# Differential attention: the low queries' score product as two row tiles, and a reordered finish of the attention outputs

## The chip, the cores and the metric

The kernel runs on one core of one Trainium2 chip. Its time is the device time in microseconds (us) of that core for one execution. A core has five engines with queues of their own that run at the same time and wait for each other through semaphores: TensorE (PE in the profile; its weight loads are listed apart as PEld), VectorE (DVE), ScalarE (ACT), GpSimd (POOL) and SyncE (SP), which here issues all DMAs.

## The reference

One layer of a hybrid block over 1024 latent tokens and 256 context tokens of width 1024: a modulated RMS norm, one wide input projection, a gated linear attention (GLA), a differential attention, and a merge with an output projection. The change lies in the differential attention, 8 heads of 2 x 64 query and key channels and 128 value channels:

```python
s1 = einsum('bhqd,bhkd->bhqk', qb1, k1) * scale      # d = 64, 1280 keys
s2 = einsum('bhqd,bhkd->bhqk', qb2, k2) * scale
a = softmax(s1) - lam * softmax(s2)
o = einsum('bhqk,bhkv->bhqv', a, v)                  # 128 value channels
...
b = rms_norm(o_diff) * diff_gain * (1 - lam_init) * silu(diff_gate)
```

Each of the two score maps of a head is called a component below (comp 0 and 1).

## The kernel before

**Split numbers.** A float32 operand is split into a high part of type fp32r and a low part, the rest. A product of two split operands is three matmuls: high x high, high x low and low x high (`mm3`). For the scores the contraction is only 64 deep, so the 128 rows of the array hold both parts of the keys: rows 0 to 63 the high part, rows 64 to 127 the low part, and the same query part stands in both halves. Two matmuls then give (Kh + Kl)Qh and (Kh + Kl)Ql. `score` in `att_scores` issues them for j = 0 (high queries) and j = 1 (low queries).

**A unit.** The attention runs over 64 units: 8 heads (hd) by 8 blocks of 128 queries (qt). For each unit `att_scores` issues, for each component, two blocks of 512 keys (`MAIN`) with two matmuls each, and for both components together one block of 256 keys each (`TAIL`), again two matmuls each: 8 matmuls of 128x512 and 4 of 128x256. They write the PSUM tile `s5`. Then `att_max` takes the row maximum on DVE, `att_exp` the exponential on ACT with the sum in `z`, and `att_mix` joins the two maps on DVE. `att_tr` transposes the result on PE, ten 128x128 transposes; `split2` makes high and low parts on ACT, POOL and DVE; `att_av` multiplies by the values for two units at a time (a pair, pr), 30 matmuls of 128x256; `att_fin` finishes a pair.

**The finish.** `att_fin` copies a pair's 128x256 output from PSUM on ACT, transposes it on PE back to tokens, squares it on ACT with a sum, multiplies it by the gate (tile `g`, loaded from `d_dg`) on DVE, works out the norm's scale (two small DVE steps, a power on POOL), scales it on DVE, transposes it again on PE, copies it on ACT and stores it to `d_bT`. Its tiles in SBUF are named `b1k`, those in PSUM `b1` (shown as `b` in the profile).

**Fill work.** `fill` runs matmuls of other products (tiles `mb` and `h`, `wt`), which the attention does not need, between the attention's own.

**Order.** Nothing is ordered by hand except the turns of scores, transposes and value products (`att_order`). A planner written in the kernel (`Driver`) simulates the engines with a cost for each operation while the program is built; generators are resumed when their operands would be ready, and the order in which they emit instructions is the order in the engines' queues. The cost of a matmul in the planner is set in `mm`.

**Keys.** `att_keys` loads a head's keys, for each component high and low part, into a ring of three slots (`kk`) of the tile `hk` (from `d_kT`), by two DMAs of 64 rows by 1280 columns. Two slots come free when a head's last unit has issued its scores.

All matmuls of `mm` carry line 349 in the profile, all transposes line 375, all DMAs line 314, and all operations of ACT, DVE and POOL line 201; so groups are told apart by their tiles.

Of the kernel before, what the change touches and what calls it, by code (L numbers as in the profile page):

```python
# [13 lines left out]
AF = mybir.ActivationFunctionType  # L14
ALU = mybir.AluOpType
# [5 lines left out]
P = 128  # L21
# [3 lines left out]
T = S + CTX  # L25
NK = D // P
EPS = 1e-6
# [205 lines left out]
class Hybrid:  # L233
# [111 lines left out]
            yield  # L345
        self.d.spawn(later(), AtPE(at), prio=-9)

    def mm(self, out, lhsT, rhs, start, stop, more=False):
        self.ins = self.nc.tensor.matmul(out, lhsT, rhs, start=start, stop=stop, skip_group_check=more).ins  # L349
        n = rhs.free_size()  # L350
        c = 0.009 + max(n, 230) * 0.000428 if rhs.dtype == F32R else 0.006 + max(4 * n, 470) / 2400
        return self.d.op("PE", c, [out], [lhsT, rhs])

    def mm3(self, out, sh, sl, mh, ml, first, last, more=False):
        self.mm(out, sh, mh, first, False, more)
# [1492 lines left out]
    def att_keys(self):  # L1848

        for hd in range(8):  # L1850
            c, x = hd // 4, hd % 4
            for i in range(10):
                yield self.ev_st["dk", c, i]
            if hd:
                yield self.ev_q[0, 1]
            else:
                yield self.gla_free[3]
                yield from self.acq("hc", 16)
                Driver.places = (T, 2 * T, 3 * T)
                self.hk = self.t("hk", [P, HK], F32R)  # L1860
            K = []
            for comp in range(2):
                rows = slice(64 * comp, 64 * comp + 64)
                yield from self.acq("kk")
                m = (2 * hd + comp) % 3
                kt = self.hk[:, m * T:(m + 1) * T]
                self.dma(kt[0:64], self.d_kT[0][c][x, rows])
                self.dma(kt[64:128], self.d_kT[1][c][x, rows])
                K.append(kt)
            self.K[hd] = K  # L1870
            self.d.set(self.ev_k[hd], self.d.when(*K))
# [68 lines left out]
    def att_scores(self):  # L1940

        nc, d = self.nc, self.d
        yield self.ev_b
        s5 = self.t("s5", [P, 2 * T])
        for hd in range(8):
            for qt in range(8):
                pr, qs = qt // 2, slice((qt % 2) * P, (qt % 2) * P + P)
                yield self.ev_k[hd]
                yield self.ev_q[hd, pr]
                K, Q = self.K[hd], self.Q[hd, pr]  # L1950

                def score(po, comp, o, n):
                    bank = po.offset % (2 * T) // 512
                    for j in range(2):
                        e = self.mm(po, Q[comp][:, j, qs], K[comp][:, o:o + n], j == 0, j == 1)
                        self.banked(self.ins, "PE", bank)
                    return e

                u = dict(hd=hd, qt=qt, E=[None, None], mt=self.t("sm", [P, 2]), mx=[self.t("sm", [P, 1]) for _ in range(2)],
                         z=self.t("sm", [P, 2]), left=2, ev=[Event() for _ in range(3)])  # L1960

                for comp in range(2):
                    yield from self.acq(f"s{comp}")
                    pm = s5[:, 1536 * comp:1536 * comp + 1024]
                    if comp == 0:
                        yield from self.turn("S", 8 * hd + qt, 0)
                    if self.flush:
                        self.flush(1)
                    for x, (o, n) in enumerate(self.MAIN[comp]):
                        e = score(pm[:, x * 512:(x + 1) * 512], comp, o, n)  # L1970
                        if x == 0:
                            yield AtPE(0)
                    self.passed("S", 8 * hd + qt, comp)
                    d.spawn(self.att_max(u["ev"][comp], u["mx"][comp], pm, 3 * comp, 3 * comp + 1), On(e, "DVE"), prio=-3)
                    yield AtPE(0)
                    if comp == 0:
                        yield from self.acq("st")
                        yield from self.turn("S", 8 * hd + qt, 1)
                        pt = s5[:, 1024:1536].rearrange("p (c k) -> p c k", c=2)
                        for x in range(2):  # L1980
                            e = score(pt[:, x], x, *self.TAIL[x])
# [36 lines left out]
    def att_mix(self, u):  # L2018
        d = self.d
        x = u["qt"] % 2  # L2020
        cf = self.t("sm", [P, 1])
        E, z = u["E"], u["z"]
        self.dve.reciprocal(cf, z[:, 1:2])
        yield On(self.dve.tensor_scalar(cf, cf, z[:, 0:1], self.nlam, ALU.mult, ALU.mult), "DVE")
        if x in self.PC:
            self.pool.tensor_scalar(E[1], E[1], cf, 0.0, ALU.mult, ALU.add)
            e = self.pool.tensor_tensor(E[0], E[0], E[1], ALU.add)
        else:
            e = self.dve.scalar_tensor_tensor(E[0], E[1], cf, E[0], ALU.mult, ALU.add)
        self.att[u["hd"], u["qt"]] = (E[0], z)  # L2030
        self.rel("e5", e)
        d.set(self.ev_a[u["hd"], u["qt"]], e)


    TAIL = ((1024, 256), (0, 256))
    MAIN = (((0, 512), (512, 512)), ((256, 512), (768, 512)))
    GROUPS = ((0, 4), (4, 4), (8, 2))
# [30 lines left out]
    def att_av(self):  # L2068
        d = self.d
        for hd in range(8):  # L2070
            for pr in range(4):
# [29 lines left out]
                d.spawn(self.att_fin(hd, pr, po, [self.att[hd, 2 * pr + x][1] for x in range(2)]), On(e, "ACT"),  # L2101
                        prio=-5 if hd == 7 and pr > 1 else self.PF)
                yield AtPE(0)

# [35 lines left out]
        self.rel("ac", e)  # L2140
        return e

    def att_fin(self, hd, pr, po, zs):
# [6 lines left out]
        ot = self.t("b1k", [P, 256])  # L2150
        e = self.act.activation(ot, po, AF.Copy)
        self.rel(self.PO, e)
        z2 = self.t("sm", [P, 2])
        for x in range(2):
            self.dve.tensor_scalar(z2[:, x:x + 1], zs[x][:, 0:1], zs[x][:, 0:1], EPS, ALU.mult, ALU.mult)
        yield AtPE(e)
        yield from self.acq("b1k")
        yield from self.acq("b1")
        pt = self.t("b1", [P, 2, P])
        for x in range(2):  # L2160
            e = self.tr(pt[:, x], ot[:, x * P:(x + 1) * P])
        self.rel("b1k", e)
        yield On(e, "ACT")
        oo = self.t("b1k", [P, 2, P])
        ss = self.t("sm", [P, 2])
        for x in range(2):
            e = self.act.activation(oo[:, x], pt[:, x], AF.Square, accum_out=ss[:, x:x + 1])
        yield d.on("DVE", pt, g)
        e2 = self.dve.tensor_tensor(g, pt, g, ALU.mult)
        self.rel("b1", max(e, e2))  # L2170
        yield On(e, "DVE")
        for x in range(2):
            self.dve.tensor_scalar(ss[:, x:x + 1], ss[:, x:x + 1], 1.0 / P, z2[:, x:x + 1], ALU.mult, ALU.add)
        yield d.on("POOL", ss)
        yield On(self.pool.tensor_tensor(ss, ss, self.nhalf[:, 0:2], ALU.pow), "DVE")
        for x in range(2):
            e = self.dve.tensor_scalar(oo[:, x], g[:, x], ss[:, x:x + 1], None, ALU.mult)
        self.rel("b1k", e)
        yield AtPE(e)
        yield from self.acq("b1k")  # L2180
        yield from self.acq("b1")
        pb = self.t("b1", [P, 2, P])
        for x in range(2):
            e = self.tr(pb[:, x], oo[:, x])
# [626 lines left out]
```

## Time and profile before

| | us |
|---|---|
| median of 3 runs | 1616.22 |
| lowest, highest | 1616.01, 1618.52 |
| span of the profiled execution | 1614.1 |
| attention with its fill work, about 890 to 1450 us of the span | 560 |
| VectorE busy in the whole span | 1224.4 (76%) |
| ScalarE busy | 835.7 (52%) |
| GpSimd busy | 634.3 (39%) |

The span is that of one execution, from its first to its last instruction. Busy times are unions: while one matmul is still draining and the next has begun, the time counts once, so TensorE can show as busy through a short wait, and a matmul's own duration (about 400 ns for 512 columns) is longer than its distance to the next one. The distance from start to start is what a matmul costs in a dense stream; it is read from the timeline or from the chain. In a row, "128\*128 128x512 f32 x496 | 138.4, 399 | 1.8" means 128 rows by 128 columns of the array in use, an output of 128x512, 496 instructions, 138.4 us busy in all, 399 ns mean of one, and 1.8 us of idle engine before them.

### The profile page before, as it was taken

The numbers are of one execution on the slowest core, as the hardware profiler recorded it, in microseconds if no ns is written. First come the engines' busy times: TensorE is split into PE (matmuls) and PEld (weight loads), VectorE is DVE, ScalarE is ACT, GpSimd is POOL, SyncE is SP. The second block draws the span as 40 slices with busy tenths as digits, with TensorE's granted clock in tenths as the row PEclk, the third lists the DMA queues.
The fourth block names the chain that finished last, engine by engine and source line by source line (L and its number), as shares of the span: only waits on it lengthen the run. The fifth ranks groups of instructions, "written<-read, shape, count | busy, mean of one in ns | idle before, by whom it ended". The sixth has DMA issues, their size and how long they took to land.

```text
span 1614.1 us, 24349 instructions
## 1 busy us (share of the span) xinstructions
PE 1591.4 (99%) x8229; PEld 1328.1 (82%) x8229; DVE 1224.4 (76%) x2118; ACT 835.7 (52%) x1720; POOL 634.3 (39%) x663
## 2 busy tenths in 40 slices
PE   8999999999999999999999999999999999999999
PEld 3788888888888888888888788888888888888887
DVE  4787945676777779767677688878778888888994
ACT  4776523435343454555535566665665666656331
POOL 1500000001415667535564256656765666560000
PEclk9999999999999999999999999999999999999999
DMA  8576996998878367564645944545587545347662
GB/s 305 201 257 239 329 304 232 344 331 295 278 238 281 116 194 235 167 212 118 189 118 158 253 121 121 151 129 151 150 264 218 159 137 150 111 155 285 204 206 100
DMA packets 259565, 331.16 MB, mean 205 GB/s; under 512 B 22600, under 2 KB 160752, under 8 KB 259440
## 3 DMA queue, kind: packets, MB, share of 16 engines
q1 hardware_dynamic: 259440, 329.60, 63.8%
q8 instruction: 65, 1.06, 0.3%
q14 instruction: 60, 0.49, 0.1%
HBM read 225.20 MB, written 104.33 MB: 204 GB/s over the span
## 4 chain that ended last, share of the span: by engine, by line
PE 89%; DVE 4%; issue 2%; DMA 2%; ACT 1%; POOL 1%; SPq 0%; ACTq 0%; DVEq 0%; POOLq 0%
PE mm L349 30%; PE mb L349 11%; PE s L349 8%; PE mc L349 7%; PE b L349 6%; PE tp L349 5%; PE gt L349 5%; PE b L375 5%; PE go L349 4%; PE gs L349 4%; PE mz L349 2%; PE tp L375 2%; DVE sm L201 1%; POOL at L201 1%; DMA w<-in_w_ada 1%
## 5 line engine op out<-in xcount | busy, mean ns | idle before, releaser
L349 PE MATMUL mm<-w,h 128*128 128x512 f32 x912 | 231.0, 400 | 0.0
L349 PE MATMUL mb<-h,wt 128*128 128x512 f32 x840 | 223.0, 400 | 0.0
L201 DVE TENSOR_REDUCE sm<-s 128x1 f32<-128x1024 f32 (+1 forms) x192 | 193.3, 1037 | 10.7 <-PE s L349 6.6
L201 ACT ACTIVATE e<-s,sm 128x1280 f32<-128x1280 f32 x128 | 169.3, 1329 | 54.4 <-DVE sm L201 51.2
L349 PEld LDWEIGHTS mm<-w,h 128*128 128x128 f32 x912 | 167.4, 188 | 32.8
L201 POOL TENSOR_TENSOR at<-ac,at 128x512 fp32r<-128x512 f32 x128 | 188.2, 1471 | 10.7
L349 PEld LDWEIGHTS mb<-h,wt 128*128 128x128 f32 x840 | 151.4, 188 | 28.6 <-DVE ft L201 0.3
L201 POOL TENSOR_SCALAR at<-ac 128x512 fp32r<-128x512 f32 x128 | 96.9, 757 | 191.0 <-ACT ac L201 190.7
L349 PE MATMUL s<-hk,aq 128*128 128x512 f32 x744 | 169.0, 363 | 1.9 <-ACT e L201 1.8
L349 PE MATMUL mm<-h,w 128*128 128x512 f32 x672 | 168.2, 400 | 1.0 <-DVE h L201 1.0
L349 PEld LDWEIGHTS mm<-h,w 128*128 128x128 f32 x672 | 123.7, 188 | 26.4 <-DVE h L201 1.5
L201 DVE TENSOR_TENSOR w<-raw,w 128x512 fp32r<-128x512 f32 x128 | 96.0, 766 | 54.2 <-ACT w L201 52.0
L349 PEld LDWEIGHTS s<-hk,aq 128*128 128x128 f32 x744 | 117.7, 189 | 18.5 <-ACT e L201 3.6
L349 PE MATMUL b<-at,vv 128*128 128x256 f32 x960 | 130.1, 287 | 1.1 <-ACT ac L201 0.8
L349 PEld LDWEIGHTS b<-at,vv 128*128 128x128 f32 x960 | 119.5, 191 | 2.8 <-ACT ac L201 1.0
L201 ACT ACTIVATE w<-raw 128x512 fp32r<-128x512 f32 x128 | 78.1, 626 | 84.2 <-PE tp L349 23.8
L201 ACT ACTIVATE ac<-b 128x512 f32<-128x512 f32 x122 | 72.5, 598 | 91.8 <-PE b L375 91.7
L201 POOL TENSOR_TENSOR sm<-sm,nhalf 128x2 f32<-128x2 f32 (+2 forms) x94 | 107.7, 1146 | 27.9 <-DVE sm L201 22.7
L201 DVE SCALAR_TENSOR_TENSOR e<-e,sm,e 128x1280 f32<-128x1280 f32 x64 | 117.9, 1842 | 1.0
L349 PE MATMUL mm<-w,g 128*128 128x512 f32 x432 | 105.7, 389 | 0.0
L349 PEld LDWEIGHTS mm<-w,g 128*128 128x128 f32 x432 | 81.1, 188 | 16.9
L375 PE MATMUL b<-ident,e 128*128 128x128 f32 x610 | 92.6, 273 | 1.3 <-ACT ac L201 0.8
(357 smaller groups left out, 3054.2 us busy)
## 6 DMA issues: line engine op xcount, KB each, us to landing
raw<-in_w_in SPq DMA_DIRECT2D x62, 512.0 KB, 4.3
g<-d_s SPq DMA_DIRECT2D x32, 640.0 KB, 6.2
g<-d_s SPq DMA_DIRECT2D x32, 512.0 KB, 5.7
aq<-d_qT SPq DMA_DIRECT2D x124, 128.0 KB, 3.4
d_dv<-pl SPq DMA_DIRECT2D x40, 256.0 KB, 3.9
gv<-d_v SPq DMA_DIRECT2D x40, 256.0 KB, 3.3
d_kT<-pl SPq DMA_DIRECT2D x40, 256.0 KB, 2.8
hk<-d_kT SPq DMA_DIRECT2D x32, 320.0 KB, 5.9
```

The lines of the kernel that those rows point to most:

```text
L201: self.ins = f(out, *args, **kw).ins
L349: self.ins = self.nc.tensor.matmul(out, lhsT, rhs, start=start, stop=stop, skip_group_check=more).ins
L375: self.nc.tensor.transpose(out, src, self.ident[:n, :n])
```

## The change

Two edits, both in the attention.

1. For each unit and component the two matmuls with the high queries come first, for both blocks of 512 keys, over all 128 rows as before. The two with the low queries use 64 rows each: the first block rows 0 to 63, the second rows 64 to 127. So that both multiply the keys' high part, `att_keys` loads high and low parts the other way round in the columns from `SWAP[comp]` on (512 for comp 0, 768 for comp 1), which makes four DMAs for two per component. The product of the low queries with the keys' low part is left out for these blocks. The planner counts the first of the two 64-row matmuls as free. The `TAIL` blocks stay as they were, with 128 rows.
2. In `att_fin` ACT copies the transposed output from PSUM to SBUF once, both squares read that copy, and one DVE step per half multiplies by scale and gate, where there was one product with the gate and two scalings. The two sums of the exponentials of a pair lie in one tile (`zp`), so two pairs of small DVE steps become one each.

```diff
-    def mm(self, out, lhsT, rhs, start, stop, more=False):
+    def mm(self, out, lhsT, rhs, start, stop, more=False, cost=1.0):
...
-        return self.d.op("PE", c, [out], [lhsT, rhs])
+        return self.d.op("PE", c * cost, [out], [lhsT, rhs])
...
-                self.dma(kt[0:64], self.d_kT[0][c][x, rows])
-                self.dma(kt[64:128], self.d_kT[1][c][x, rows])
+                for j in range(2):
+                    for h, cs in ((j, slice(0, self.SWAP[comp])), (1 - j, slice(self.SWAP[comp], T))):
+                        self.dma(kt[64 * h:64 * h + 64, cs], self.d_kT[j][c][x, rows, cs])
...
-                def score(po, comp, o, n):
-                    bank = po.offset % (2 * T) // 512
-                    for j in range(2):
-                        e = self.mm(po, Q[comp][:, j, qs], K[comp][:, o:o + n], j == 0, j == 1)
-                        self.banked(self.ins, "PE", bank)
+                def score(po, comp, o, n, j, rows=slice(0, P), cost=1.0):
+                    e = self.mm(po, Q[comp][rows, j, qs], K[comp][rows, o:o + n], j == 0, j == 1, cost=cost)
+                    self.banked(self.ins, "PE", po.offset % (2 * T) // 512)
                     return e
...
                     for x, (o, n) in enumerate(self.MAIN[comp]):
-                        e = score(pm[:, x * 512:(x + 1) * 512], comp, o, n)
+                        score(pm[:, x * 512:(x + 1) * 512], comp, o, n, 0)
                         if x == 0:
                             yield AtPE(0)
+                    for x, (o, n) in enumerate(self.MAIN[comp]):
+                        e = score(pm[:, x * 512:(x + 1) * 512], comp, o, n, 1, slice(64 * x, 64 * x + 64), float(x))
...
+    SWAP = (512, 768)
...
-        for x in range(2):
-            self.dve.tensor_scalar(z2[:, x:x + 1], zs[x][:, 0:1], zs[x][:, 0:1], EPS, ALU.mult, ALU.mult)
+        self.dve.scalar_tensor_tensor(z2, zp[:, :, 0], EPS, zp[:, :, 0], ALU.mult, ALU.mult)
...
-        oo = self.t("b1k", [P, 2, P])
-        ss = self.t("sm", [P, 2])
+        oc = self.t("b1k", [P, 2, P])
+        ss = self.t("sm", [P, 2])
+        self.rel("b1", self.act.activation(oc, pt, AF.Copy))
         for x in range(2):
-            e = self.act.activation(oo[:, x], pt[:, x], AF.Square, accum_out=ss[:, x:x + 1])
-        yield d.on("DVE", pt, g)
-        e2 = self.dve.tensor_tensor(g, pt, g, ALU.mult)
-        self.rel("b1", max(e, e2))
+            e = self.act.activation(ot[:, x], oc[:, x], AF.Square, accum_out=ss[:, x:x + 1])
...
-        for x in range(2):
-            self.dve.tensor_scalar(ss[:, x:x + 1], ss[:, x:x + 1], 1.0 / P, z2[:, x:x + 1], ALU.mult, ALU.add)
+        self.dve.scalar_tensor_tensor(ss, ss, 1.0 / P, z2, ALU.mult, ALU.add)
...
         for x in range(2):
-            e = self.dve.tensor_scalar(oo[:, x], g[:, x], ss[:, x:x + 1], None, ALU.mult)
+            e = self.dve.scalar_tensor_tensor(oc[:, x], oc[:, x], ss[:, x:x + 1], g[:, x], ALU.mult, ALU.mult)
```

More of the change, by code (lines that the diff above doesn't have):

```diff
@@ L1950, in att_scores @@
                 K, Q = self.K[hd], self.Q[hd, pr]
-                def score(po, comp, o, n):
-                    bank = po.offset % (2 * T) // 512
-                    for j in range(2):
-                        e = self.mm(po, Q[comp][:, j, qs], K[comp][:, o:o + n], j == 0, j == 1)
-                        self.banked(self.ins, "PE", bank)
-                    return e
+                def score(po, comp, o, n, j, rows=slice(0, P), cost=1.0):
+                    e = self.mm(po, Q[comp][rows, j, qs], K[comp][rows, o:o + n], j == 0, j == 1, cost=cost)
+                    self.banked(self.ins, "PE", po.offset % (2 * T) // 512)
+                    return e
+                if qt % 2 == 0:
+                    zp = self.t("sm", [P, 2, 2])
                 u = dict(hd=hd, qt=qt, E=[None, None], mt=self.t("sm", [P, 2]), mx=[self.t("sm", [P, 1]) for _ in range(2)],
-                         z=self.t("sm", [P, 2]), left=2, ev=[Event() for _ in range(3)])
+                         z=zp[:, qt % 2], zp=zp, left=2, ev=[Event() for _ in range(3)])
                 for comp in range(2):
@@ L1980, in att_scores @@
                         for x in range(2):
-                            e = score(pt[:, x], x, *self.TAIL[x])
+                            for j in range(2):
+                                e = score(pt[:, x], x, *self.TAIL[x], j)
                         d.spawn(self.att_max(u["ev"][2], u["mt"], pt, 2), On(e, "DVE"), prio=-3)
@@ L2029, in att_mix @@
             e = self.dve.scalar_tensor_tensor(E[0], E[1], cf, E[0], ALU.mult, ALU.add)
-        self.att[u["hd"], u["qt"]] = (E[0], z)
+        self.att[u["hd"], u["qt"]] = (E[0], u["zp"])
         self.rel("e5", e)
         d.set(self.ev_a[u["hd"], u["qt"]], e)
+    SWAP = (512, 768)
     TAIL = ((1024, 256), (0, 256))
@@ L2100, in att_av @@
                     self.rel("vv", e, 2)
-                d.spawn(self.att_fin(hd, pr, po, [self.att[hd, 2 * pr + x][1] for x in range(2)]), On(e, "ACT"),
+                d.spawn(self.att_fin(hd, pr, po, self.att[hd, 2 * pr][1]), On(e, "ACT"),
                         prio=-5 if hd == 7 and pr > 1 else self.PF)
@@ L2141, in split2, with att_fin @@
         return e
-    def att_fin(self, hd, pr, po, zs):
+    def att_fin(self, hd, pr, po, zp):
         nc, d = self.nc, self.d
@@ L2149, in att_fin @@
             "(c p) e -> p c e", p=P))
-        ot = self.t("b1k", [P, 256])
-        e = self.act.activation(ot, po, AF.Copy)
+        ot = self.t("b1k", [P, 2, P])
+        e = self.act.activation(ot.rearrange("p x t -> p (x t)"), po, AF.Copy)
         self.rel(self.PO, e)
         z2 = self.t("sm", [P, 2])
-        for x in range(2):
-            self.dve.tensor_scalar(z2[:, x:x + 1], zs[x][:, 0:1], zs[x][:, 0:1], EPS, ALU.mult, ALU.mult)
+        self.dve.scalar_tensor_tensor(z2, zp[:, :, 0], EPS, zp[:, :, 0], ALU.mult, ALU.mult)
         yield AtPE(e)
@@ L2160, in att_fin @@
         for x in range(2):
-            e = self.tr(pt[:, x], ot[:, x * P:(x + 1) * P])
+            e = self.tr(pt[:, x], ot[:, x])
+        yield On(e, "ACT")
+        oc = self.t("b1k", [P, 2, P])
+        ss = self.t("sm", [P, 2])
+        self.rel("b1", self.act.activation(oc, pt, AF.Copy))
+        for x in range(2):
+            e = self.act.activation(ot[:, x], oc[:, x], AF.Square, accum_out=ss[:, x:x + 1])
         self.rel("b1k", e)
-        yield On(e, "ACT")
-        oo = self.t("b1k", [P, 2, P])
-        ss = self.t("sm", [P, 2])
+        yield On(e, "DVE")
+        self.dve.scalar_tensor_tensor(ss, ss, 1.0 / P, z2, ALU.mult, ALU.add)
+        yield d.on("POOL", ss)
+        yield On(max(self.pool.tensor_tensor(ss, ss, self.nhalf[:, 0:2], ALU.pow), d.when(g)), "DVE")
         for x in range(2):
-            e = self.act.activation(oo[:, x], pt[:, x], AF.Square, accum_out=ss[:, x:x + 1])
-        yield d.on("DVE", pt, g)
-        e2 = self.dve.tensor_tensor(g, pt, g, ALU.mult)
-        self.rel("b1", max(e, e2))
-        yield On(e, "DVE")
-        for x in range(2):
-            self.dve.tensor_scalar(ss[:, x:x + 1], ss[:, x:x + 1], 1.0 / P, z2[:, x:x + 1], ALU.mult, ALU.add)
-        yield d.on("POOL", ss)
-        yield On(self.pool.tensor_tensor(ss, ss, self.nhalf[:, 0:2], ALU.pow), "DVE")
-        for x in range(2):
-            e = self.dve.tensor_scalar(oo[:, x], g[:, x], ss[:, x:x + 1], None, ALU.mult)
+            e = self.dve.scalar_tensor_tensor(oc[:, x], oc[:, x], ss[:, x:x + 1], g[:, x], ALU.mult, ALU.mult)
         self.rel("b1k", e)
@@ L2183, in att_fin @@
         for x in range(2):
-            e = self.tr(pb[:, x], oo[:, x])
+            e = self.tr(pb[:, x], oc[:, x])
         self.rel("b1k", e)
```

## The prediction

> **What bounds the kernel now.** I read the page's busy shares, clock and chain first, then the attention's stretch.
>
> ```profile
> PE 1591.4 (99%) x8229; PEld 1328.1 (82%) x8229; DVE 1224.4 (76%) x2118; ACT 835.7 (52%) x1720; POOL 634.3 (39%) x663
> ...
> PE 89%; DVE 4%; issue 2%; DMA 2%; ACT 1%; POOL 1%; SPq 0%; ACTq 0%; DVEq 0%; POOLq 0%
> ```
>
> TensorE is busy 99% of the span and makes 89% of the chain that ended last. A busy PE may still hide waits, so the stretch itself has to be seen. The columns of the windows view are the stretch, then busy time and count of PE, PEld, DVE, ACT and POOL, the granted clock and the DMAs.
>
> ```profile
> 890.00:1450.00 560.00, 553.12 (x3354) 479.38 (x3353) 459.24 (x839) 336.18 (x688) 343.32 (x307) 1.00 0.56 161
> ...
> L349 PE MATMUL s<-hk,aq 128*128 128x512 f32 x496 | 138.4, 399 | 1.8 <-ACT e L201 1.8
> L349 PE MATMUL s<-hk,raw 128*128 128x512 f32 x16 | 4.6, 406 | 0.5 <-ACT e L201 0.3 <-ACT p L201 0.3
> ...
> PE s L349 <- ACT e L201: 2.0, 3, 1.3
> PE b L375 <- DVE b1k L201: 1.8, 4, 0.7
> ```
>
> In those 560 us PE idles 6.9 us, DVE is busy 82%, ACT 60%, POOL 61%; the clock is granted whole. The 496 + 16 = 512 main score matmuls are all there (64 units x 8). Their longest waits sum to 2 us. What one costs in the dense stream shows in the chain of work inside the stretch (start, length, what):
>
> ```profile
> 1006.71 0.93 PE s L349 x4
> ...
> 1012.65 3.44 PE mb L349 x15
> ...
> 1016.78 2.32 PE s L349 x12
> 1019.10 0.44 PE b L375 x4
> 1019.54 2.15 PE b L349 x18
> ```
>
> Four main score matmuls back to back take 0.93 us: **0.2325 us** each. Fill matmuls (mb) take 0.229, value products (b, 18) 0.119, transposes 0.11. The pieces lie end to end: this stage is PE's stream, and what leaves the stream leaves the time, as fill work (mb) is there to close what opens.
>
> **The change, part by part.**
>
> *Row tiles.* Each unit and component has two low-query matmuls of 0.2325 us. If the two 64-row ones run beside each other, one is gone: 64 x 2 = 128 times at most 0.2325 = **29.8 us**. Against that stand two costs that no row shows directly: the second tile's weights, and going from 128 rows to 64 and back.
>
> Weight loads after a pause show how fast loads can follow each other:
>
> ```profile
> 910.99 0.19 PEld L349 LDWEIGHTS s<-hk,aq 128*128 128x128 f32 x1 [1.76 <-ACT e L201]
> ...
> 911.10 0.19 PEld L349 LDWEIGHTS s<-hk,aq 128*128 128x128 f32 x1
> ...
> L349 PE MATMUL s<-hk,aq 128*128 128x512 f32 x1 | 0.5, 499 | 1.3 <-ACT e L201 1.3
> ```
>
> The second load starts 0.11 us after the first, and the matmul whose load had no cover takes 499 ns where the mean is 399: an uncovered load costs about 0.10 us. Two loads take 0.22 us and so fit behind one 512-wide matmul (0.2325), if the second may be loaded that early; then the pair costs one matmul. If it may start only with the first tile's matmul, the pair costs 0.2325 + 0.11 = 0.34. So the gain of a pair lies between 0.12 and 0.2325 us, 15.7 to 29.8 us in all. I take the middle, 0.178 x 128 = **22.7 us**, as neither load order is in the trace.
>
> The switch of shapes has rows on both sides. Early in the kernel matmuls with 4 columns follow some with 128:
>
> ```profile
> 31.57 0.84 PE L349 MATMUL mm<-h,w 128*128 128x512 f32 x3
> 32.25 0.40 PE L349 MATMUL gs<-w,cs 128*4 128x512 f32 x1
> ```
>
> Three matmuls from 31.57 to 32.25 are 0.227 each: fewer columns cost no pause. Fewer rows stand only in front of a few transposes, here the timeline of loads, then of matmuls:
>
> ```profile
> 24.36 0.32 PEld L375 LDWEIGHTS gt<-ident,p 2*128 2x128 f32 x4 [0.66 <-DVE p L201]
> 24.70 0.64 PEld L375 LDWEIGHTS tp<-ident,g 128*128 128x128 f32 x6
> ...
> 24.37 0.40 PE L375 MATMUL gt<-ident,p 2*128 2x2 f32 x4 [0.57 <-DVE p L201]
> 24.70 0.76 PE L375 MATMUL tp<-ident,g 128*128 128x128 f32 x5
> ...
> 46.10 0.33 PE L375 MATMUL tp<-ident,g 128*128 128x128 f32 x1
> ...
> L375 PE MATMUL gt<-ident,p 2*128 2x2 f32 x3 | 0.3, 196 | 0.0
> ...
> L375 PE MATMUL tp<-ident,g 128*128 128x128 f32 x1 | 0.3, 328 | 0.0
> ...
> L375 PE MATMUL b<-ident,e 128*128 128x128 f32 x1 | 0.3, 329 | 0.8 <-ACT ac L201 0.8
> ```
>
> The last 2-row matmul (196 ns, ending at 24.37 + 0.40 = 24.77) starts at 24.57; the 128-row load comes at 24.70, about 0.125 us later and 0.02 after the loads before it ended (24.36 + 0.32). In the second such place (46.10) the first 128-row transpose takes 328 ns, as much as one after 0.8 us of idle (329): the way back to 128 rows began like a standing start. These matmuls have almost nothing to stream, so two readings fit. If the 0.125 us count from the last matmul's start, a 512-wide one covers them: 0.125 + 0.10 for the load = 0.225, under 0.2325; **a switch costs nothing**. If they count from the end of its stream, which for 512 columns lasts (0.2325 - 0.119) x 2 = 0.227, the next matmul starts 0.227 + 0.125 + 0.10 = 0.45 after the last, **0.22 more per switch**, twice per pair. I take the first: it is what the clocked distance says as it stands, and the column switch shows that a new shape alone does not stop the stream. The second is rival 1.
>
> Here the Trainium skill speaks against the change: "TensorEngine Tiling (Array Packing)", Key Properties, says that a change of tiling mode, unlike a change of tile, drains TensorE. The column rows above contradict it for columns, the row-tile exits look like it. By that rule the 22.7 us would become the loss of rival 1. On the other side, "TensorE: Matmul & The Clock Gate", Part 3, has matmuls in different row tiles start about 4 ns apart, with loads overlapping when the row groups differ; the sum by it, an estimate, would be 128 x 0.2285 = 29 us. No row here has two row tiles side by side.
>
> *Keys.*
>
> ```profile
> hk<-d_kT SPq DMA_DIRECT2D x32, 320.0 KB, 5.9
> ...
> L314 SPq DMA_DIRECT2D hk<-d_kT x27: 460/588/1730, 916.8 to 1356.3; - x27
> ```
>
> 32 issues become 64 of half the size: 32 x 0.588 = 19 us more on SP's queue, two more issues (1.2 us) per component ahead of the landing of 5.9 us, and the loads of `aq`, `vv` and `b1k` queue behind them. Cost: nothing, hidden by transposes, value products and fill that PE runs around a head's first scores; the waits of PE name no DMA. Without that cover 7 heads x 1.2 = 8.4 us.
>
> *Finish.* DVE and ACT, 32 pairs:
>
> ```profile
> L201 DVE TENSOR_SCALAR sm<-sm,sm 128x1 f32<-128x1 f32 x190 | 32.5, 206 | 0.7
> L201 DVE TENSOR_SCALAR b1k<-b1k,sm 128x128 f32<-128x128 f32 x62 | 26.1, 463 | 29.7 <-POOL sm L201 29.7
> L201 DVE TENSOR_TENSOR b1k<-b,b1k 128x256 f32<-128x256 f32 x31 | 12.8, 413 | 0.0
> L201 DVE TENSOR_SCALAR sm<-sm 128x1 f32<-128x1 f32 x62 | 10.1, 203 | 0.0
> L201 DVE SCALAR_TENSOR_TENSOR gp<-go,sm,gp 128x256 f32<-128x256 f32 x2 | 0.9, 480 | 5.5 <-POOL sm L201 5.5
> ...
> L201 ACT ACTIVATE b1k<-b 128x256 f32<-128x256 f32 x62 | 24.1, 388 | 26.3 <-PE b L375 21.6 <-PE b L349 4.3
> L201 ACT ACTIVATE b1k<-b 128x128 f32<-128x128 f32 x62 | 16.7, 277 | 24.1 <-PE b L375 24.1
> ```
>
> DVE now does 2 x 0.203 + 2 x 0.206 + 0.413 + 2 x 0.463 = 2.16 us a pair. After: two small steps at 0.206, and two 128x128 steps with gate, between 0.206 (a step with nothing to stream) and 0.480 (the same operation at twice the width); I keep 0.463, the row of the step replaced. That is 1.34, so 0.82 x 32 = 26 us less on DVE. ACT gains one copy, 0.388 x 32 = 12.4 us; squares from SBUF I leave at 277, the bound being the 0.277 itself. Both lie beside PE, on engines busy 82% and 60%: worth nothing in the sum. What PE does wait for is this chain's end (b1k, 1.8 us in 4 waits). The copy puts 0.39 before the squares, the gate's product takes 0.41 out behind them; between all 1.8 us gone and 0.39 more at 32 finishes (12.5 us if the planned order left no room) I take 0, as 28 of the 32 finishes make PE wait for nothing.
>
> With DVE at 459 - 26 = 433 us of a stage of 560 - 23 = 537, its share falls to 81%: no new bound.
>
> **Sum:** 1614.1 - 22.7 = 1591.4 for the profiled execution, which lies 2.1 under the median of the runs; against that median **1593.5 us**.
>
> **Rivals.**
>
> 1. *Both switches drain (slower).* At each of 128 pairs PE waits 0.22 before and 0.22 after: + 0.43 - 0.2325 + 0 to 0.11 for the second load = + 0.20 to + 0.31 us a pair, + 26 to + 40: **1642 to 1656**. It decides from 0.116 us a switch on. For it: the standing start at 24.70 and 46.10. Against it: that those matmuls had no stream to cover a load.
> 2. *Only the way back drains.* -0.2325 + 0.22 + 0 to 0.11 = -0.01 to + 0.10 us a pair: **1614 to 1629**. For it: only that direction is in the trace.
> 3. *The tiles don't run beside each other.* Then PE has as many matmuls of 0.2325 as before: **1613 to 1619** with the finish's 1.8 us and the run spread. Nothing in the trace shows two at once.
> 4. *The gain is there and partly lost*, to keys landing late (8.4) or finishes in PE's way (up to 12.5): **1601 to 1612**. Against it: PE's waits are short now.
>
> **How the numbers follow.** Forecast (1584 to 1601, the row tiles' 15.7 to 29.8 and up to 1.8 from the finish) 0.56; rival 1 0.20; rival 2 0.10; rival 3 0.08; rival 4 0.06. About 0.2%, 3 us, is what a measurement of this kernel can tell from no change. Faster: forecast and rival 4, 0.62, and 0.01 of rival 3: 0.63. Same: 0.06 of rival 3 and 0.03 of rival 2: 0.09. Slower: rival 1, 0.07 of rival 2, 0.01 of rival 3: 0.28. The range leaves out rival 1 and holds the rest: 1584 to 1629; the forecast's own is 1584 to 1601.
>
> **What would show it.** Right: in the chain, a component's four main matmuls near 0.70 to 0.81 us instead of 0.93, starts of the two 64-row ones 0 to 0.11 apart, the next 128-row load within 0.13 of the second one's start, and a stage some 23 us shorter. Wrong: that load 0.3 us or more after it, first 128-row matmuls near 499 ns (a drain); starts 0.23 apart (no overlap); waits of PE for DMAs of `hk` or for `b1k` that weren't there. DVE should be some 26 us less busy and ACT 12 more with the time unmoved by it.

## The result and the profile after

The changed kernel is slower: 1643.14 us median (1639.42 to 1644.18, 4 runs) beside 1617.37 for the kernel before on the same chips, a ratio of 1.0153 with a 95% interval of 1.0138 to 1.0168. The prediction said 1593.5 us, range 1584 to 1629: wrong in its sign. The profiled execution has a span of 1641.3 us, 27.2 more than before.

From the page of the changed kernel, the engines' busy time and the chain that ended last:

```profile
PE 1611.9 (98%) x8229; PEld 1296.9 (79%) x8229; DVE 1237.4 (75%) x2022; ACT 850.6 (52%) x1752; POOL 633.0 (39%) x663
...
PE 91%; DVE 3%; DMA 2%; ACT 2%; issue 1%; POOL 1%; SPq 0%; ACTq 0%; DVEq 0%; POOLq 0%
```

TensorE bounds it as before. The attention's stretch, with the columns of the windows view as before, ends some 25 us later:

```profile
890.00:1475.00 585.00, 572.80 (x3353) 447.19 (x3353) 470.93 (x745) 351.05 (x720) 339.21 (x305) 0.99 0.52 154
...
1475.00:1641.30 166.30, 162.43 (x733) 134.40 (x731) 132.98 (x216) 65.51 (x124) 3.44 (x4) 1.00 0.60 203
```

PE idles 12.2 us in it where it was 6.9, and DVE has 471 us of work where 459 were and 433 were forecast. The rest of the loss is in PE's own stream. The groups by shape, PE's and the weight loads':

```profile
L349 PE MATMUL s<-hk,aq 128*128 128x512 f32 x248 | 79.7, 402 | 2.5 <-ACT e L201 2.5
L349 PE MATMUL s<-hk,aq 64*128 64x512 f32 x248 | 62.3, 499 | 0.0
...
L349 PEld LDWEIGHTS s<-hk,aq 64*128 64x128 f32 x248 | 23.2, 184 | 45.3 <-issue 45.3
```

The 64-row matmuls take 499 ns each, the duration that the trace of before showed for a matmul whose weight load had no cover, and the shortest of all 256 takes 491. They are 62.3 us busy for 248, half of 499: the two of a pair lie on top of each other. In front of their loads the load path stands idle 45.3 us with nothing that released it ("issue"): 0.37 us for each pair.

One pair in the timeline, loads first, then matmuls (start, length). The view joins neighbours with the same tiles under the first one's shape, so the x3 at 1002.16 are the last 128-row matmul and both 64-row ones:

```profile
1001.45 0.67 PEld L349 LDWEIGHTS s<-hk,aq 128*128 128x128 f32 x5
1002.49 0.19 PEld L349 LDWEIGHTS s<-hk,aq 64*128 64x128 f32 x2 [0.36 <-issue]
1002.92 0.42 PEld L375 LDWEIGHTS b<-ident,e 128*128 128x128 f32 x4 [0.25 <-issue]
...
1002.16 0.83 PE L349 MATMUL s<-hk,aq 128*128 128x512 f32 x3
1002.92 0.55 PE L375 MATMUL b<-ident,e 128*128 128x128 f32 x3
```

The last 128-row matmul starts at 1002.16. Both 64-row loads come at 1002.49, 0.33 later, together (two loads in 0.19 us, the length of one). The next 128-row load comes at 1002.92, 0.43 later. Over all 128 pairs the medians are 325 ns from the last 128-row matmul to the first 64-row load, 3 ns between the two loads and between the two matmuls, and 430 ns from the pair to the next 128-row load. So **the tiles run beside each other, and PE stops at both changes of shape**.

### The profile page after: what moved, and what is told of

Its sections match the earlier page's. It is cut to its first block, busy times and chain, and to the rows that moved or that the text cites. A ratio compares the mean times of both kernels' runs of the same rounds, so it can differ in the third digit from the quotient of the medians.

```text
span 1641.3 us, 24351 instructions
## 1 busy us (share of the span) xinstructions
PE 1611.9 (98%) x8229; PEld 1296.9 (79%) x8229; DVE 1237.4 (75%) x2022; ACT 850.6 (52%) x1752; POOL 633.0 (39%) x663
## 4 chain that ended last, share of the span: by engine, by line
PE 91%; DVE 3%; DMA 2%; ACT 2%; issue 1%; POOL 1%; SPq 0%; ACTq 0%; DVEq 0%; POOLq 0%
PE mm L349 30%; PE mb L349 12%; PE s L349 8%; PE mc L349 7%; PE b L349 6%; PE tp L349 6%; PE b L375 5%; PE gt L349 5%; PE go L349 4%; PE gs L349 4%; PE mz L349 2%; PE tp L375 2%; DVE sm L201 1%; DMA w<-in_w_ada 1%; DMA raw<-in_w_in 1%
## 5 line engine op out<-in xcount | busy, mean ns | idle before, releaser
L349 PE MATMUL mb<-h,wt 128*128 128x512 f32 x840 | 227.5, 408 | 0.7 <-DVE ft L201 0.6
L201 POOL TENSOR_TENSOR at<-ac,at 128x512 fp32r<-128x512 f32 x128 | 197.3, 1542 | 10.7
L201 POOL TENSOR_SCALAR at<-ac 128x512 fp32r<-128x512 f32 x128 | 101.2, 791 | 206.7 <-ACT ac L201 180.9
L349 PEld LDWEIGHTS s<-hk,aq 128*128 128x128 f32 x744 | 94.2, 189 | 58.6 <-issue 45.5
L201 POOL TENSOR_TENSOR sm<-sm,nhalf 128x2 f32<-128x2 f32 (+2 forms) x94 | 101.8, 1083 | 37.6 <-DVE sm L201 32.4
L201 DVE SCALAR_TENSOR_TENSOR e<-e,sm,e 128x1280 f32<-128x1280 f32 x64 | 113.3, 1770 | 0.9
```

The source lines that it names most:

```text
L201: self.ins = f(out, *args, **kw).ins
```

## The experiments

A way to take PE's account helps to read all of them. From the first score matmul to the end PE has 2048 matmuls of 512 columns, 1216 of 256 and 768 transposes; at their distances in a dense stream, 0.2305, 0.119 and 0.109 us, these are 700.5 us. With pairs counted as one slot they are 671.0. What the trace shows beyond that is called stops here. It also holds some 4 us behind PE's last matmul, alike in all runs, and what a lowered clock takes (3.4 us in the changed kernel, 1.7 in e3 and e9, nothing in before, e1, e2 and e6). Worked out from each trace:

| run | first score to end | slots | stops | of it visible idle of PE |
|---|---|---|---|---|
| before | 715.4 | 700.5 | 14.9 | 6.9 |
| changed kernel | 740.8 | 671.0 | 69.9 | 12.4 |
| e1_tiles_only | 735.4 | 671.0 | 64.5 | 6.5 |
| e6_full_cost | 736.6 | 671.0 | 65.6 | 8.7 |
| e2_finish_only | 720.3 | 700.5 | 19.9 | 12.2 |
| e3_all_rows | 726.8 | 700.5 | 26.3 | 14.6 |
| e9_layout_order | 722.3 | 700.5 | 21.8 | 10.1 |
| e14_split_key | 715.6 | 700.5 | 15.1 | 6.9 |

### The two halves of the change

**e1_tiles_only** is the changed kernel with `att_fin` and the tile of the sums as they were before:

```diff
-    def att_fin(self, hd, pr, po, zp):
+    def att_fin(self, hd, pr, po, zs):
...
-                         z=zp[:, qt % 2], zp=zp, left=2, ev=[Event() for _ in range(3)])
+                         z=self.t("sm", [P, 2]), left=2, ev=[Event() for _ in range(3)])
```

> The changed kernel with the finish of before; only the row tiles are left. Theory A (the switches between 128 and 64 rows cost the time): the changed kernel shows the first 64-row load 325 ns after the last 128-row matmul's start and the next 128-row load 430 ns after the pair's start; with 0.10 us for an uncovered load that makes 0.325 + 0.43 + 0.105 = 0.86 us from the last 128-row matmul with high queries to the next one after the pair, where three matmuls of 0.2325 took 0.70: + 0.163 us x 128 = + 21 us. So 1636 to 1644. Theory B (the finish, whose DVE steps became longer instead of shorter, costs it): within 3 us of before, 1614 to 1620. Theory C (both): about half of the loss, 1626 to 1634.

1637.88 us, ratio 1.0126 (1.0112 to 1.0140), + 20.8, within theory A's range. The stops rise by 64.5 - 14.9 = 49.6 us at nearly the same visible idle (6.5 for 6.9), and there are 256 changes of shape: **0.194 us each**. The distances of the trace give the same in another way: (0.325 - 0.2325) beyond the usual distance and 0.105 for the uncovered load (499 ns for a mean of 394 to 399) are 0.198. 49.6 lost and 29.5 of slots saved make + 20.1.

**e2_finish_only** is the kernel before with the new finish. 

> The kernel before with the changed finish only. Theory A (switches): within 3 us of before, 1614 to 1620, since PE still sets the time. Theory B (finish): 1635 to 1645, all of the loss. Theory C: 1621 to 1632. In all cases DVE's two gate-and-scale steps should stay near the 777 ns a piece that the changed kernel shows (463 before) if it is their operands that make them long; if they come back to 463 or less, it was the crowding with the row tiles' stage.

1624.04 us, ratio 1.0038 (1.0025 to 1.0050), + 6.9, in theory C's range: most of the loss is the tiles', but the finish, with the order that comes with it, is not free. Both together make 27.7, about the whole loss of 25.8.

### Taking the row mode away, and the second tile

**e3_all_rows** keeps everything, but both low products use 128 rows; the orders of PE, DVE, ACT and POOL are those of the changed kernel.

```diff
-                        e = score(pm[:, x * 512:(x + 1) * 512], comp, o, n, 1, slice(64 * x, 64 * x + 64), float(x))
+                        e = score(pm[:, x * 512:(x + 1) * 512], comp, o, n, 1, slice(0, P), float(x))
```

> The changed kernel with the low queries' products over all 128 rows again (the low-by-low product is back in), and all else kept: the key layout, the finish, the planner's costs, and with them the order of every queue but a few DMA issues. It takes away the row mode alone. Theory A (switches): PE has 128 more matmul slots of 0.2325 us but no switch: 1643 - 21 = 1622, down to 1617 if the longer waits of the stage (12.2 us of idle PE for 6.9) come from PE running late against the plan as well; range 1616 to 1625. Theory B (finish, keys or order): stays at 1638 to 1648, or rises by 128 x 0.2325 = 30 us to 1673 if the row tiles as such had gained what was forecast.

1627.86 us, ratio 1.0063 (1.0050 to 1.0077): 15.3 less than the changed kernel, though PE has 128 slots more; between the ranges of both theories. The row mode loses by itself: at the same order the stops fall by 69.9 - 26.3 = 43.6 us, **0.17 us** for each of the 256 changes of shape. Of the 5.7 us that are missing of the 21, 2.2 lie in PE's visible idle (14.6 us for 12.4); where the rest lies is not shown.

**e4_one_group** puts both low matmuls of a pair into rows 0 to 63; the keys' high part stands there in all columns.

```diff
-                        e = score(pm[:, x * 512:(x + 1) * 512], comp, o, n, 1, slice(64 * x, 64 * x + 64), float(x))
+                        e = score(pm[:, x * 512:(x + 1) * 512], comp, o, n, 1, slice(0, 64), float(x))
...
-                    for h, cs in ((j, slice(0, self.SWAP[comp])), (1 - j, slice(self.SWAP[comp], T))):
+                    for h, cs in ((j, slice(0, self.SWAP[comp])), (j, slice(self.SWAP[comp], T))):
```

> The changed kernel with both low-query matmuls of a pair in rows 0 to 63 (the keys' high part stands there in all columns). Same number of switches, same order, but the two can't lie in different row tiles. If the tiles of the changed kernel do run beside each other, as starts 3 ns apart say, a pair takes one more slot: 128 x 0.2325 = + 30 us, 1673 (1666 to 1680). If the second load is not covered either, 128 x 0.33 = + 43, 1686. If the 3 ns are only how the trace writes it down and the pair runs one after the other already, the time stays at 1638 to 1648.

1667.13 us, + 24.0 on the changed kernel: the gain of the second tile is real. A pair in its timeline, loads and then matmuls:

```profile
1000.00 0.29 PEld L349 LDWEIGHTS s<-hk,aq 64*128 64x128 f32 x2 [0.36 <-issue]
...
1000.00 0.73 PE L349 MATMUL s<-hk,aq 64*128 64x512 f32 x2
```

Two loads now take 0.29 us, 0.11 apart, and the pair 0.73 us where side by side it is 0.50: 0.23 x 128 = 29 us, of which less visible idle (7.9 for 12.4) gives 4.5 back.

### Fewer changes of shape

**e5_two_pairs** takes e1's finish and puts both components' pairs behind all 128-row scores of a unit, so that 128 changes of shape are left of 256, and tells the planner their cost. The main part of its edit:

```diff
+                for comp in range(2):
+                    for x, (o, n) in enumerate(self.MAIN[comp]):
+                        e = score(pms[comp][:, x * 512:(x + 1) * 512], comp, o, n, 1, slice(64 * x, 64 * x + 64), self.LOW[comp][x])
...
+    LOW = ((0.87, 1.0), (0.0, 1.87))
```

> Row tiles with the finish of before (as the run with the tiles alone, 1637.9), but both components' pairs of 64-row matmuls stand together at the end of a unit, so a unit goes to 64 rows and back once, not twice; the planner is told the switch. Theory A (each switch costs (0.325 - 0.2325) + 0.105 = 0.198 us): 64 units x 2 switches x 0.198 = 25 us less than with the tiles alone: 1612.6, that is 4.5 under before (two matmuls of 0.2325 saved a unit for 0.395). Later row maxima may give back a few us: 1611 to 1620. Theory A' (the cost lies in the 64-row matmuls themselves, not in the change of shape): stays at 1633 to 1642.

1671.20 us, ratio 1.0334 (1.0320 to 1.0348): neither theory's number. The price per change holds: over all 64 units the medians are 327 ns into the 64 rows and 324 out of them (the changed kernel's 430 holds the 105 ns of its pair's uncovered load as well). One unit's timeline:

```profile
1011.11 0.30 PEld L349 LDWEIGHTS s<-hk,aq 64*128 64x128 f32 x4 [0.24 <-issue]
1011.77 0.20 PEld L375 LDWEIGHTS b<-ident,e 128*128 128x128 f32 x2 [0.37 <-ACT b1k L201]
...
1011.45 0.40 PE L349 MATMUL s<-hk,aq 64*128 64x512 f32 x2
1011.78 0.33 PE L375 MATMUL b<-ident,e 128*128 128x128 f32 x1
```

All four loads go within 0.30 us, the second pair starts 0.34 after the first (0.23 and the uncovered load) with 0.40 us a matmul, the usual length: inside one shape nothing stops. What failed is the schedule around it. Both components' maxima and exponentials now start late together, and PE waits for them:

```profile
PE s L349 <- ACT e L201: 12.1, 19, 1.1
PE b L375 <- ACT ac L201: 8.8, 11, 1.1
...
1480.00:1530.00 50.00, 37.41 (x182) 30.60 (x181) 31.93 (x62) 19.64 (x50) 16.07 (x15) 0.83 0.46 152
```

PE idles 39 us from the first score on, and in five stretches between 1431 and 1520 its granted clock is 0.50 (from 1480 to 1530 that makes 0.83 in the mean). Of those stretches PE was busy 26.7 us, so the clock takes another 13.4. The stops are 768.0 - 671.0 = 97.0 us; without idle and clock 44.5 are left, where e1 has 58.0. That is 13.5 us less of the 25 expected: it points the right way, but the gain of half the changes was not shown as time.

**e12_two_pairs_spread** tried to mend that by another order of turns:

```diff
-            order += T(o) + S(o + lead) + [t[0], a[0], t[1], a[1], s[0], t[2], s[1]]
+            order += T(o) + S(o + lead) + [a[0], t[0], t[1]] + s + [a[1], t[2]]
```

> One way into the row tiles and back per unit, as in the run of two pairs (1671.2, whose PE idled 36 us, mostly for exponentials, and whose clock fell to 0.987), but with the turns spread so that transposes and value products stand between any two units' scores. Theory A (0.198 us a switch) gives 1612.6 where the waits are those of before; with 20 us of idle PE left it is 1627; so 1611 to 1630. Theory A' (no gain from half the switches): 1638 or more with less than 15 us of idle PE.

1808.07 us, ratio 1.1182 (1.1167 to 1.1197): a miss. PE waits 57.5 us for the finish's tiles on ACT, 31.9 for small DVE steps, 23.6 for ACT's copies, and the mean clock is 0.958. Each change costs as before (medians of 327 and 323 ns), but what half the changes gain doesn't show.

**e6_full_cost** is e1 with the planner told 0.87 and 1.87 matmuls for a pair. 

> The tiles alone (1637.9) with the planner told the cost measured: 0.87 and 1.87 matmuls for the two of a pair instead of 0 and 1. If the loss is the switches on PE, nothing is to be had from another order: 1634 to 1641. If part of it is the plan that believed PE to be 0.4 us a pair faster, it falls by more than 4 us, under 1634.

1638.99 us: nothing comes back. With quite another order the stops are 65.6 us, (65.6 - 14.9) / 256 = 0.198 per change, or 0.191 without the 1.8 us that PE idles longer than before.

**e9_layout_order** keeps only the key layout and the order high, high, low, low, with 128 rows and full costs:

```diff
-                        e = score(pm[:, x * 512:(x + 1) * 512], comp, o, n, 1, slice(64 * x, 64 * x + 64), float(x))
+                        e = score(pm[:, x * 512:(x + 1) * 512], comp, o, n, 1)
```

> The tiles alone (1637.9) with the low queries' products over all 128 rows again and counted in full by the planner: the key layout, its four DMAs and the order high, high, low, low remain of the change, with the finish of before. If the row mode alone makes the loss: within 3 us of before (1617.0), 1614 to 1620, and the row mode costs 1637.9 less this, about 21 us. If keys that land later or the new order cost part: 1621 to 1630.

1624.75 us, ratio 1.0043 (1.0027 to 1.0059), + 7.4, not the 3 allowed for. No wait of PE names a key DMA; PE waits 3.3 us for `b1k` and 2.7 for `ac` (before 1.8 and 0.8). The layout or the moved order costs something; the run doesn't part them.

### The finish

**e7_small_steps** has only the merged small steps and the shared tile of the sums, **e8_copy_gate** only the ACT copy, the squares from SBUF and the step with scale and gate.

```diff
-        for x in range(2):
-            self.dve.tensor_scalar(z2[:, x:x + 1], zs[x][:, 0:1], zs[x][:, 0:1], EPS, ALU.mult, ALU.mult)
+        self.dve.scalar_tensor_tensor(z2, zp[:, :, 0], EPS, zp[:, :, 0], ALU.mult, ALU.mult)
```

> The kernel before with one part of the finish only: the two pairs of one-wide small DVE steps as one two-wide step each, with two tensors from SBUF. Finish as a whole: 1624.0, + 6.9. If the small steps' new waits (mean 432 and 596 ns for 203 and 206 in the run with the finish alone, up to 1258) carry it: + 3 to + 7, 1620 to 1624. If the copy and the gate step carry it: within 2 us of before, 1615 to 1619.

> The complement: ACT copy, squares from SBUF, scale with gate in one DVE step, small steps as before. If copy and gate carry the finish's + 6.9: 1621 to 1625. If the small steps do: within 2 us of before, 1615 to 1619. Both parts alike would be 1619 to 1622 in either run.

e7: 1627.04 us, + 10.1. e8: 1618.45 us, ratio 1.0003 (0.9994 to 1.0012). The copy and the gate step cost nothing, with an order of PE that differs from before's as much as e9's does: another order is not always a loss. The small steps with the shared tile cost more than the whole finish.

**e10_two_tensors** leaves tiles and counts as before, but writes the four small steps with two tensors from SBUF:

```diff
-            self.dve.tensor_scalar(z2[:, x:x + 1], zs[x][:, 0:1], zs[x][:, 0:1], EPS, ALU.mult, ALU.mult)
+            self.dve.scalar_tensor_tensor(z2[:, x:x + 1], zs[x][:, 0:1], EPS, zs[x][:, 0:1], ALU.mult, ALU.mult)
```

> The kernel before with its four small one-wide DVE steps of a finish written as steps on two tensors in SBUF (same results, same number of instructions, same cost to the planner, tiles as before). The small steps of the change cost + 10.1 us (1627.0). If the waits of such steps behind GpSimd's operations (up to 1258 ns for 0.205) make that: 1622 to 1630, with four of them instead of two even more. If not: 1615 to 1619, with the small steps' mean still well over 0.3 us each.

1622.28 us, ratio 1.0030 (1.0019 to 1.0040), + 5.0: half of e7's loss, where more was expected. The order is nearly that of before (8020 of PE's 8229 instructions stand in the same sequence). Its tile view of `sm` (count, then min/median/max in ns), and two timelines of the same moment, DVE's and POOL's:

```profile
L201 DVE TENSOR_SCALAR sm<-sm,sm x128: 194/205/216, 904.5 to 1431.3; 128x1 f32<-128x1 f32 x128
...
L201 DVE SCALAR_TENSOR_TENSOR sm<-sm x64: 144/152/1277, 936.0 to 1458.4; 128x1 f32<-128x1 f32 x64
L201 DVE SCALAR_TENSOR_TENSOR sm<-sm,sm x64: 144/150/1276, 941.3 to 1467.9; 128x1 f32<-128x1 f32 x64
...
982.22 1.34 DVE L201 SCALAR_TENSOR_TENSOR sm<-sm,sm 128x1 f32<-128x1 f32 x2
...
982.22 1.33 POOL L201 TENSOR_TENSOR at<-ac,at 128x512 fp32r<-128x512 f32 x1
```

The one-wide step with one tensor never takes more than 216 ns. The one with two takes 144 at best and up to 1277, and the long ones end with a GpSimd operation: of the two here the second lasts from 982.29 to 983.56, and POOL's operation ends at 983.55. All 30 that last over 300 ns end within 24 ns of one.

**e11_shared_tile** shares the tile of the sums and changes nothing else; **e14_split_key** shares it too, but lets the planner keep a time of readiness for each half, which gives PE, ACT and DVE the order of before.

```diff
+                if qt % 2 == 0:
+                    zp = self.t("sm", [P, 2, 2])
...
-                         z=self.t("sm", [P, 2]), left=2, ev=[Event() for _ in range(3)])
+                         z=zp[:, qt % 2], left=2, ev=[Event() for _ in range(3)])
```

```diff
+        if x.name in Driver.pairs:
+            return x.name + "ab"[ap is not x and ap.offset % 4 >= 2]
```

> The kernel before with the sums of a pair of units in one tile, as the change has them, and nothing else; the small steps stay one-wide with one tensor. If the shared tile makes the + 10.1 us of the small steps (the planner keeps one time of readiness per tile, so it holds the first unit's steps back for the second's, and the queues are ordered otherwise): 1622 to 1630. If the steps themselves do: 1615 to 1619.

> The shared tile of the sums (1626.7, + 9.4), with the planner keeping its two halves apart; the queues of PE, ACT and DVE then have the order of before. If real waits between the units of a pair cost the 9.4 us: 1623 to 1628. If the planner's false dependence and the order it leads to do: back at before, 1615 to 1619.

e11: 1626.73 us, + 9.4. e14: 1617.30 us, ratio 0.9994 (0.9986 to 1.0003). All five queues of e14 have the order of before. So the shared tile costs nothing on the chip; **the order that the planner lays out for it costs 9.4 us**. e7 has the same tile, so its + 10.1 isn't the price of its steps alone; its order is neither before's nor e11's, and how it divides stays open.

**e13_plan_nudge** changes one constant of the planner, and no work:

```diff
-                c = 0.07 + 0.055 * scalars + n * 0.00104 * (
+                c = 0.075 + 0.055 * scalars + n * 0.00104 * (
```

> The kernel before, with the planner's fixed cost of a DVE step raised from 0.070 to 0.075 us and nothing else: same instructions, another order (some 1165 lines of PE's queue moved). If another order by itself costs some us around a well-kept order, as the runs with few changes suggest: 1619 to 1630. If orders are alike and only work counts: within 2 us of before, 1615 to 1619.

1638.89 us, ratio 1.0129 (1.0115 to 1.0143): + 20.6 us from the order alone, more than the 1619 to 1630 expected. Its first score comes 14.3 us later (913.0 for 898.8), and from there to the end it takes 8.0 more (723.4). Only the 8.0 compare with the other runs: their PE order is that of before up to the first scores.

**e15_finish_split** is e2 with the halves kept apart. 

> The finish alone (1624.0, + 6.9) with the planner keeping the halves of the shared tile apart. If the shared tile's order made the finish's cost: 1615 to 1620, no faster than before, since DVE and ACT stand beside PE. If the two-tensor DVE steps' waits do: 1621 to 1626.

1637.08 us, ratio 1.0111 (1.0096 to 1.0126): wrong both ways. PE waits 14.8 us for `b1k` in 13 places (before 1.8 in 4), its visible idle is 21.5 us. A likely reason, not tested: the planner counts a step of scale with gate at 0.26 us and a small one at 0.07, by its formula, and the run with the finish alone shows means of 0.695 and of 0.432 and 0.596, so the order is laid out for steps that end earlier than they do.

No version beat the kernel before.

## Why the prediction was wrong

**What bounds the kernel** was read rightly: PE's stream is the path, and what was saved or added there came through one to one (29.5 saved, 49.6 added, + 20.8 measured for the tiles alone). What failed are the prices of two terms, the switch and the finish, and the order, which the sum doesn't have.

**The tiles side by side, and the second load**: right, and better than the middle I took. The loads start 3 ns apart, so a pair saves its whole 0.23, not 0.178. The estimate from the Trainium skill ("TensorE: Matmul & The Clock Gate", Part 3: about 4 ns between starts in different row tiles) agrees with this case's 3 ns.

**The switch of shapes is the step that failed.** From the 0.125 us between a 2-row matmul and the next load I took the reading by which the count runs from the matmul's start and a 512-wide one covers it. The runs show the other reading: 325 ns, where it would have given 227 + 125 = 352 and mine 125, and then the load lies open. I took a switch at nothing, and priced it at 0.22 us as rival 1; it measured 0.17 (e3, the order kept), 0.194 (e1) and 0.198 (e6). Rival 1's 26 to 40 us is thus 20.8 here, its lower end less the 6 us by which the switch was dearer in the estimate. The range that I gave left rival 1 out. The evidence was quoted: a first matmul of 328 ns after the change, as after idle. I set against it that fewer *columns* didn't stop the stream, which says nothing on rows. The rule of the Trainium skill that I weighed ("TensorEngine Tiling (Array Packing)", Key Properties: a change of mode drains TensorE) agrees with this case for rows, 325 ns and 430 ns at 128 pairs. I read the row of before with 4 columns, 0.227 us apart, as contradicting it for columns. That was too strong: the rule speaks of modes, and no run here shows whether a matmul of 4 columns is in another mode at all.

With these numbers the change could not win as built: a pair saves 0.23 and its two changes cost 0.39. That only the way back drains (rival 2) and that the tiles don't overlap (rival 3) are both refuted by the same timeline.

**Keys**: as predicted, no wait of PE names their DMAs in the changed kernel. What the layout costs apart from the order that came with it stays open; e9's + 7.4 holds both.

**Finish**: taken as nothing on the path and 26 us less on DVE. DVE got 13.0 us more in the whole span (1237.4 for 1224.4), ACT 14.9 for the 12 forecast, and PE's waits for `b1k` on DVE rose from 1.8 to 4.3 us. The steps with two tensors are the mis-sized term: the changed kernel's rows, for 0.206 and 0.463 expected:

```profile
L201 DVE SCALAR_TENSOR_TENSOR b1k<-b1k,sm,b1k 128x128 f32<-128x128 f32 x62 | 45.7, 777 | 9.7 <-DMA b1k<-d_dg 5.2 <-POOL sm L201 4.5
...
L201 DVE SCALAR_TENSOR_TENSOR sm<-sm 128x2 f32<-128x2 f32 x31 | 16.6, 537 | 0.0
L201 DVE SCALAR_TENSOR_TENSOR sm<-sm,sm 128x2 f32<-128x2 f32 x31 | 11.7, 376 | 3.1 <-ACT b1k L201 3.1
```

The Trainium skill states why ("SBUF — State Buffer", SBUF: two separate sides): a VectorE operation with two SBUF inputs and a GpSimd operation that reads SBUF exclude each other for a whole instruction. The moment at 982.22 agrees, and so do all 30 long steps of e10. I priced these steps by rows with one tensor and never asked what GpSimd does meanwhile. The row of 463 was itself a mean of two kinds, as the tile view of before shows (min/median/max):

```profile
L201 DVE TENSOR_SCALAR b1k<-b1k,sm x64: 273/286/1341, 942.7 to 1464.7; 128x128 f32<-128x128 f32 x64
```

20 of these 64 steps last over 600 ns, and all 20 end 79 to 86 ns after a GpSimd operation. So a 128x128 step with one tensor waits as well, and its mean of 463 is no price of the step alone.

**The order** is missing from the prediction. I allowed for waits at the finishes but took the planner's order as given, where any change of a cost or of a tile makes another one. e13 shows + 8.0 us from the first score on for such a change without work, and e11 + 9.4, so the finish's + 6.9 can't be put down to its work: e8 has most of that work, in an order of its own, at no cost, and e14 has the shared tile at no cost. How much of e2's 6.9 is the DVE waits (e10: + 5.0, with a nearly kept order) and how much the order stays open. The tiles' + 20.8 is not such chance: e3 takes the row mode away at the same order of PE, DVE, ACT and POOL, in e1 and e6 two different orders give nearly the same price per change of shape, and the trace shows it at each pair.

## What to carry to other kernels

A pair of half-height matmuls saves one slot, and going to another row shape and back costs about 0.39 us here: count the changes of shape first. By these numbers row tiles need at least two pairs between the changes to gain anything; no run here shows that gain as time. Price an operation by a row with the same operands, not only the same size, and look at its median and its longest beside the mean: a second SBUF tensor made a one-wide VectorE step wait for GpSimd here, 150 ns in the median and up to 1277. In a kernel whose order comes from a planner, a control that changes only the order belongs beside every measurement of an edit, before a per cent is put down to it.

## What the runs showed of the hardware

- A change between 128 and 64 rows stops TensorE in both directions: 0.17 to 0.20 us each (e3, e1, e6) beside a stream of 512-wide matmuls. Inside the 64-row shape (e5) a second pair starts 0.34 us after the first, 0.23 and the first's uncovered load, and its own loads are covered.
- Loads and matmuls in two row tiles start 3 ns apart; in the same rows (e4) the second load comes 0.11 us and the second matmul 0.34 us after the first.
- After idle PE the granted clock halved for 3.4 us. In the changed kernel PE waits 0.58 us for `e` and 1.62 and 0.88 us for `b1k`, idle 3.1 of 6.8 us, and right behind it:

```profile
1181.34 0.30 PE L375 MATMUL b<-ident,b1k 128*128 128x128 f32 x1 [1.62 <-DVE b1k L201]
1182.52 0.33 PE L375 MATMUL b<-ident,b1k 128*128 128x128 f32 x1 [0.88 <-DVE b1k L201]
...
1176.00:1182.80 6.80, 3.71 (x19) 2.37 (x18) 3.56 (x6) 4.09 (x7) 5.04 (x5) 1.00 0.93 258
1182.80:1186.20 3.40, 3.40 (x14) 2.31 (x13) 3.25 (x7) 1.83 (x3) 0.00 (x0) 0.50 1.05 405
1186.20:1190.00 3.80, 3.80 (x31) 3.62 (x30) 3.37 (x6) 2.56 (x6) 2.68 (x2) 1.00 1.06 387
```

The two 64-row matmuls in the stretch at clock 0.50 take 791 ns, for 499 elsewhere: such waits cost their own length and up to 1.7 us more, half of 3.4. How much idle it takes is not worked out here: a second such stretch of the same run, from 1360.3 on, had one visible wait of 1.63 us ahead of it.
